# Samples' scores in halves of two units, eleven buffers of gathered latents, and rotary gathers queued behind the latents' gathers

## The chip, the core and the metric

The kernel runs on one core of a Trainium2 chip: TensorE (PE in the profile, its weight loads PEld), VectorE (DVE), ScalarE (ACT), GpSimd (POOL), SyncE (SP) and sixteen DMA engines. The metric is device time in microseconds; less is better. The kernel before took 1371.54 us (median of three runs, 1371.13 to 1372.58).

## The reference

One inference step of a two-layer decoder for a prompt of 1024 tokens (and 16 meta tokens) and for eight requests of four new tokens each ("samples"). The samples attend to a paged cache of 2048 past positions each. For a request, with its pages gathered by the page table:

```python
q_lat = einsum('blhd,chd->blhc', q_nope, w_uk)          # 16 heads x 4 tokens = 64 rows, 256 latent columns
keys  = concat([past_c, past_kr])                       # 256 latent + 32 rotary columns, 2048 positions
s     = (q_lat . latents + q_rope . rotary keys) * SCALE
p     = softmax(s)
o_lat = p @ latents                                     # 64 x 256
o     = einsum('blhc,chv->blhv', o_lat, w_uv)
y     = x + rmsnorm((o * silu(z)) @ w_out_mla)
```

The prompt goes through the same layer with ordinary keys and values, and both streams share the output weights. Everything is float32; the kernel splits each operand into a rounded high part and the rest, and multiplies high x high, high x low and low x high.

## The kernel before

The program is traced in Python and then put in order by a scheduler, which runs a simulation of the engines and, on each engine, takes the instruction that is ready, earliest in program order first. A tile can be allocated only when a buffer of its tag is free. Pools stand one behind the other in each partition of the on-chip memory; a pool opened after another was closed takes the same bytes, and its instructions wait for the last use of what lay there.

The prompt's attention ends near 1105 us. Its pool `wq` (L669) holds per partition: `raw` 2 x 6144 bytes, `ph` (tag wh) 4 x 2048, and `pl` (tag wl) 4 x 2048. `ph` and `pl` are the high and low part of the probabilities (`parts`, L1195), made for each unit of each head and read by `values` (L1213) three units later, to the last unit of the last head.

The samples' stage begins at L1306. Pool `sc` (7424 bytes) takes the bytes from where `wq` began; then stand, in this order, `sw`, `sg`, `sk`, `sch`, `scn0`, `sn` and `scn1`:

- `sw` (22592 bytes): `ot` 1024, the scores `st` 2 x 8192, `m` 2 x 32, `pt` 2 x 2560.
- `sg` (768 bytes): the page table (L1318), `crow`, `ktab`, `krow`, `krun`: the rows to gather. The page table is one load (L1319), `ktab` eight (L1328); VectorE makes `krow` (L1330) and `crow` (L1333) of them.
- `sk`: `kn`, `kx`, `kh`, `kl` (one buffer each) and `kp` (five): gathered rotary keys, transposed, split, and moved to the layout of a matmul.
- `scn0` and `scn1`: `cn`, the gathered latents, 3 and 6 buffers of 4096 bytes.

The work is 32 units: request b, quarter g of its positions (512 of them). The loop (L1545) goes in steps; at step s it calls

- `gather` (L1393) of unit s+5: an indirect DMA issued by GpSimd, 512 KB into `cn`;
- `rotary` (L1374) of the request whose first unit is s+4: an indirect DMA into `kn`, and SyncE's twelve DMAs to `kp`;
- `take` (L1399) of unit s+1: eight transposes on TensorE, split by ScalarE (`ch`) and VectorE (`cl`);
- `scores` (L1414) of unit s: five matmuls, the one with `kp` among them, and VectorE's sum into `st`; after the fourth unit of a request `softmax` (L1426);
- `turn` and `halve` (L1438, L1457) of unit s-5, `weigh` (L1467) of unit s-6: the probabilities transposed (`pt`), the latents split (`nh`, `nl`, after which `cn` is free), eight matmuls; `close` (L1482) ends a request;
- and, from step 5 on, a share of `left` (L1522): the prompt's rows times the first half of the output weights, with its `gh` queued on ScalarE behind the latest `ch`. `columns` (L1502) loads and splits those weights through two `raw` buffers; `left` copies its product to `ma` and stores it.

The gathers and the rotary gathers go through `spread` (L1367), which puts each behind a later mask instruction of the last two heads on GpSimd. After the loop `uv` is loaded into a buffer of `st`, and the second half of the output weights follows (L1589).

## Time and profile before

| | |
|---|---|
| median of the runs | 1371.54 us |
| profiled execution | 1369.06 us, of which its span is 1367.3 |
| TensorE busy | 94% of the span (weight loads 85%) |
| VectorE, ScalarE, GpSimd busy | 63%, 49%, 45% |
| mean granted clock of TensorE | 0.975 of 2.4 GHz |

A row of a timeline gives the start and the length in us, the engine, the line, the operation, what it writes and reads, the count of merged instructions, and in brackets how long the engine was idle before it and what ended that. A row of busy time by stretch gives, for each engine, busy us and instructions. All times count from the start of the span.

### The profile page before, as it was taken

The page shows a single profiled execution, that of the slowest core. Times are in us where ns is not written, and L with a number is a line of the kernel's source. Part 1 is how long each engine was busy: PE and PEld are TensorE (multiplying, and loading weights), DVE is VectorE, ACT ScalarE, POOL GpSimd, SP SyncE. Part 2 cuts the span into 40 slices and gives each one's busy share as a digit, 9 for nine tenths or more (in the row PEclk, how much of TensorE's full clock was granted, in tenths as well). Part 3 has the DMA queues.
Part 4 walks back from the last instruction along what each step waited for, and adds up shares of the span by engine and source line. Part 5 has one row for each costly group of instructions (what it writes and reads, how often), then busy time and mean ns, then how long its engine had stood idle before and what let it go on. Part 6 is the DMA issues. An engine that isn't in the chain of part 4 may idle for free.

```text
span 1367.3 us, 22924 instructions
## 1 busy us (share of the span) xinstructions
PE 1291.8 (94%) x8142; PEld 1163.4 (85%) x8142; DVE 854.9 (63%) x1749; ACT 673.8 (49%) x1394; POOL 609.3 (45%) x828
## 2 busy tenths in 40 slices
PE   7799999999989999999999989999999879899988
PEld 6699999999968899999999878878888757677776
DVE  5776555666464445167523667777778669567875
ACT  5433333333243334222321566666767668678842
POOL 5456555555311133463410654655546634445421
PEclk8999999999999999999999999999999979999999
DMA  6122122122362232345610121121211276444354
GB/s 194 46 64 72 48 70 79 49 78 63 100 214 93 91 109 69 99 150 197 214 41 1 40 63 36 36 63 28 61 35 38 73 213 182 114 146 134 105 183 168
DMA packets 107149, 131.86 MB, mean 96 GB/s; under 512 B 21135, under 2 KB 80187, under 8 KB 107035
## 3 DMA queue, kind: packets, MB, share of 16 engines
q1 hardware_dynamic: 101787, 111.51, 27.6%
q0 software_dynamic: 5248, 18.88, 4.5%
q8 instruction: 65, 1.06, 0.3%
q14 instruction: 49, 0.40, 0.1%
HBM read 93.95 MB, written 28.78 MB: 90 GB/s over the span
## 4 chain that ended last, share of the span: by engine, by line
PE 74%; DMA 10%; DVE 6%; ACT 3%; issue 3%; POOL 2%; SPq 1%; DVEq 0%; POOLq 0%; ACTq 0%
PE b L69 11%; PE pa L69 10%; PE po L69 8%; PE ps L69 8%; PE c L69 7%; PE a L69 6%; PE pm L69 6%; PE pz L69 6%; DMA qh<-qd32h 3%; PE pf L69 3%; PE pr L69 3%; PE pc L1406 2%; DMA cn<-in_cache_ckv_dram,crow 1%; PE pk L69 1%; PE pt L69 1%
## 5 line engine op out<-in xcount | busy, mean ns | idle before, releaser
L79 DVE TENSOR_TENSOR wl<-raw,wh 128x512 fp32r<-128x512 f32 x86 | 70.6, 823 | 85.4 <-ACT wh L74 82.2
L74 ACT ACTIVATE wh<-raw 128x512 fp32r<-128x512 f32 x88 | 55.2, 630 | 127.7 <-PE pa L69 48.9
L1187 ACT ACTIVATE p<-ps 128x512 f32<-128x512 f32 (+1 forms) x192 | 93.4, 492 | 37.5 <-PE ps L69 33.7
L74 ACT ACTIVATE ph<-p 128x512 fp32r<-128x512 f32 (+1 forms) x192 | 97.5, 527 | 22.0 <-POOL p L1192 20.6
L69 PE MATMUL pz<-ph,v 128*128 128x512 f32 (+3 forms) x384 | 104.4, 358 | 0.4 <-ACT ph L74 0.2
L79 POOL TENSOR_TENSOR nl<-cn,nh 128x256 fp32r<-128x256 f32 x64 | 60.3, 959 | 87.3 <-ACT nh L74 63.2
L79 POOL TENSOR_TENSOR pl<-p,ph 128x512 fp32r<-128x512 f32 (+2 forms) x75 | 81.8, 1099 | 31.5 <-ACT ph L74 23.5
L79 DVE TENSOR_TENSOR pl<-p,ph 128x512 fp32r<-128x512 f32 (+3 forms) x117 | 79.1, 681 | 26.5 <-ACT ph L74 24.7
L1043 DVE TENSOR_REDUCE mx<-pm 128x1 f32<-128x16 f32 (+6 forms) x210 | 83.5, 424 | 18.9 <-PE pm L69 18.5
L1192 POOL TENSOR_SCALAR_AFFINE_SELECT p<-p 128x127 f32<-128x127 f32 (+1 forms) x128 | 48.3, 381 | 82.7 <-ACT p L1187 65.1
L69 PEld LDWEIGHTS pz<-ph,v 128*128 128x128 f32 x384 | 65.8, 192 | 7.2 <-ACT ph L74 1.2
L69 PE MATMUL pm<-kh,qh 128*128 128x144 f32 (+6 forms) x210 | 61.3, 342 | 11.0 <-DMA qh<-qd32h 10.8
L69 PE MATMUL ps<-qh,kh 97*128 97x512 f32 (+3 forms) x192 | 68.8, 358 | 2.5 <-ACT p L1187 1.3
L69 PE MATMUL pz<-pl,v 128*128 128x512 f32 (+1 forms) x192 | 68.0, 355 | 2.3 <-DVE pl L79 2.1
L69 PE MATMUL ps<-qh,kl 97*128 97x512 f32 (+3 forms) x192 | 67.5, 351 | 0.0
L69 PE MATMUL ps<-ql,kh 97*128 97x512 f32 (+3 forms) x192 | 67.3, 351 | 0.0
L69 PE MATMUL pa<-x1h,wh 128*128 128x352 f32 x288 | 64.5, 331 | 0.0
L69 PE MATMUL pa<-x1h,wl 128*128 128x352 f32 x288 | 63.9, 328 | 0.0
L69 PE MATMUL pa<-x1l,wh 128*128 128x352 f32 x288 | 62.9, 327 | 0.0
L74 ACT ACTIVATE wh<-s 128x512 fp32r<-128x512 f32 x48 | 30.0, 630 | 66.5 <-POOL s L173 25.9
L108 POOL TENSOR_SCALAR ta<-ss 128x1 f32<-128x1 f32 (+2 forms) x36 | 9.3, 257 | 118.8 <-ACT xa L623 51.7
L79 DVE TENSOR_TENSOR wl<-s,wh 128x512 fp32r<-128x512 f32 x45 | 44.4, 989 | 20.5 <-ACT wh L74 18.8
(483 smaller groups left out, 4418.7 us busy)
## 6 DMA issues: line engine op xcount, KB each, us to landing
raw<-in_w_in_conv_dram SPq DMA_DIRECT2D x32, 512.0 KB
raw<-in_w_in_mla_dram SPq DMA_DIRECT2D x12, 512.0 KB
raw<-in_w_out_conv_dram SPq DMA_DIRECT2D x8, 512.0 KB
x1d<-xa SPq DMA_DIRECT2D x8, 512.0 KB
qd64h<-qxh SPq DMA_DIRECT2D x8, 512.0 KB
qd64l<-qxl SPq DMA_DIRECT2D x8, 512.0 KB
qh<-qd64h SPq DMA_DIRECT2D x16, 256.0 KB
ql<-qd64l SPq DMA_DIRECT2D x16, 256.0 KB
```

Source lines behind the costliest of these rows:

```text
L69: return pe.matmul(out, a, b, start=start, stop=stop, **kw)
L74: return act.activation(out, src, AF.Copy, scale=scale)
L79: (eng or dve).tensor_tensor(out, src, f(hi), ALU.subtract)
L108: pool.tensor_scalar(t[:r], ss[:r], 1.0 / n, EPS, ALU.mult, ALU.add)
L1043: dve.tensor_reduce(mx[:, b, c:c + 1], pm[:, :off], AX.X, ALU.max)
L1187: act.activation(pt[:r, :n], ps[:r, :n], AF.Exp, scale=SCALE)
L1192: marks[h] = marks.get(h, []) + [pool.affine_select(pt[:r, :dn], pt[:r, :dn], [[1, dn]], ALU.is_ge, 0.0, base=META + c0 - t * P, channel_m ...
L1406: state["turned"] = pe.transpose(pc[:, r], cn[:, r, c * P:(c + 1) * P], ident)
```

## The change

The scores of a request are kept in two tiles of two units, from three buffers of half the size, in place of one tile of four units from two buffers; `softmax` and `turn` index them so, and `uv` is loaded in two halves into two of them. The latents' buffers are 3 and 8 in place of 3 and 6. From request 2 on, the rotary gather is queued on GpSimd behind the latents' gather that was traced last. The tile `ma` of `left` shares the tag, and so the two buffers, of the weights' `raw`.

```diff
--- before.py
+++ after.py
@@ -1311,9 +1311,10 @@
         sg = l9.enter_context(sbuf("sg"))
         sk = l9.enter_context(sbuf("sk"))
         sch = l9.enter_context(sbuf("sch"))
-        scn = [l9.enter_context(sbuf("scn0", bufs=CNB[0]))]
+        cnb = 3, 8
+        scn = [l9.enter_context(sbuf("scn0", bufs=cnb[0]))]
         sn = l9.enter_context(sbuf("sn"))
-        scn.append(l9.enter_context(sbuf("scn1", bufs=CNB[1])))
+        scn.append(l9.enter_context(sbuf("scn1", bufs=cnb[1])))
 
         table = sg.tile([P, NB, PAGES // 4, 4], I32, name="table")
         sp.dma_start(table.rearrange("p b g n -> p (b g n)"), i["page_table"].rearrange("b p -> (b p)").rearrange("(a n) -> a n", a=1).to_broadcast((P, NB * PAGES)))
@@ -1335,7 +1336,7 @@
         kruns = i["cache_krope"].rearrange("n (k r) d -> (n k) (r d)", r=16)
 
         def fetch(dst, src, row):
-            pool.indirect_dma_start(dst, None, src, bass.IndirectOffsetOnAxis(ap=row, axis=0))
+            return pool.indirect_dma_start(dst, None, src, bass.IndirectOffsetOnAxis(ap=row, axis=0))
 
         rr_ = sc.tile([2 * DR + 4, SEQ], F32R, tag="olt", name="rr")[2 * DR:]
         divisors(pairs[NH // 2 - 1], new, rr_)
@@ -1369,12 +1370,15 @@
             n = len(fetched) * SPN
             fetched.append(n)
             with tc.issue_after(order[min(n, len(order) - 1)]):
-                fetch(*args)
+                return fetch(*args).ins
 
         def rotary(b):
 
             kn = sk.tile([P, 16, DR], F32, tag="kn", name="kn", bufs=1)
-            spread(kn.rearrange("p r d -> p (r d)"), kruns, krow[:, b:b + 1])
+            with ExitStack() as l:
+                if b > 1:
+                    l.enter_context(tc.issue_after(state["g"]))
+                spread(kn.rearrange("p r d -> p (r d)"), kruns, krow[:, b:b + 1])
             kx = sk.tile([P, 4, 4, 32], F32, tag="kx", name="kx", bufs=1)
             dve.transpose(kx.rearrange("p a r k -> p (a r k)"), kn.rearrange("p r d -> p (r d)"))
 
@@ -1391,9 +1395,9 @@
                 state["p", b, g] = kp
 
         def gather(b, g):
-            pl = scn[(4 * b + g) % sum(CNB) >= CNB[0]]
+            pl = scn[(4 * b + g) % sum(cnb) >= cnb[0]]
             cn = pl.tile([P, 4, KV], F32, tag="cn", name="cn")
-            spread(cn.rearrange("p r c -> p (r c)"), cruns, crow[:, b, g:g + 1])
+            state["g"] = spread(cn.rearrange("p r c -> p (r c)"), cruns, crow[:, b, g:g + 1])
             state["n", b, g] = cn
 
         def take(b, g):
@@ -1419,31 +1423,31 @@
 
             t = sch.tile([DN, 512], F32, tag="t", name="t", bufs=2)
             act.activation(t, ps[DN:], AF.Copy)
-            if g == 0:
-                state["s", b] = sw.tile([P, 4, 512], F32, tag="st", name="st")
-            dve.tensor_tensor_reduce(state["s", b][:DN, g], ps[:DN], t, 1.0, NEG, ALU.add, ALU.max, tops[:, b, g:g + 1])
+            if g % 2 == 0:
+                state["s", b, g // 2] = sw.tile([P, 2, 512], F32, tag="st", name="st", bufs=3)
+            dve.tensor_tensor_reduce(state["s", b, g // 2][:DN, g % 2], ps[:DN], t, 1.0, NEG, ALU.add, ALU.max, tops[:, b, g:g + 1])
 
         def softmax(b):
-            st = state["s", b]
             m = sw.tile([DN, 2], F32, tag="m", name="m")
             dve.tensor_reduce(m[:, 0:1], tops[:, b], AX.X, ALU.max)
             dve.tensor_scalar(m[:, 1:2], m[:, 0:1], -SCALE, None, ALU.mult)
             mine = own[:, (TS + LS) * b:(TS + LS) * b + LS]
             act.activation(mine, fresh[:, b], AF.Exp, scale=SCALE, bias=m[:, 1:2], accum_out=sums[:, b, 0:1])
             for n in range(2):
-                act.activation(st[:DN, 2 * n:2 * n + 2], st[:DN, 2 * n:2 * n + 2], AF.Exp, scale=SCALE, bias=m[:, 1:2], accum_out=sums[:, b, n + 1:n + 2])
+                st = state["s", b, n]
+                act.activation(st[:DN], st[:DN], AF.Exp, scale=SCALE, bias=m[:, 1:2], accum_out=sums[:, b, n + 1:n + 2])
             dve.tensor_reduce(sums[:, b, 3:4], sums[:, b, :3], AX.X, ALU.add)
             dve.reciprocal(sums[:, b, 3:4], sums[:, b, 3:4])
 
         def turn(b, g):
 
-            st = state["s", b]
+            st = state["s", b, g // 2]
             if b == NB - 1:
                 pp = pss.tile([P, 512], F32, tag="s", name="pp")[:, :5 * DN].rearrange("p (n c) -> p n c", c=DN)
             else:
                 pp = psp.tile([P, 5, DN], F32, tag="p", name="pp")
             for n in range(4):
-                pe.transpose(pp[:, n], st[:DN, g, n * P:(n + 1) * P], ident[:DN, :DN])
+                pe.transpose(pp[:, n], st[:DN, g % 2, n * P:(n + 1) * P], ident[:DN, :DN])
             pt = sw.tile([P, 5, P], F32R, tag="pt", name="pt", bufs=PTB)
             if g == 3:
                 pe.transpose(pp[:TS, 4], own[:, TS * b:TS * b + TS], ident[:DN, :DN])
@@ -1529,7 +1533,7 @@
                     mm(po[:r], x[:, k, :r], w[k], k == 0 and n == 0, k == NK - 1 and n == 2)
                 if k % 2:
                     yield
-            a = nw.tile([P, 512], F32, tag="a", name="ma", bufs=2)
+            a = nw.tile([P, 512], F32, tag="raw", name="ma", bufs=2)
             act.activation(a[:r], po[:r], AF.Square, scale=D ** -0.5, accum_out=ss2[:r, b, 0:1])
             pool.tensor_scalar(ss2[:r, b, 2:3], ss2[:r, b, 0:1], EPS, None, ALU.add)
             act.activation(a[:r], po[:r], AF.Copy)
@@ -1567,12 +1571,13 @@
             while done < (s_ - FS) * FR:
                 next(fill, None)
                 done += 1
-        uv = sw.tile([P, 4, 512], F32, tag="st", name="uv").rearrange("p (c a) m -> p c (a m)", c=2)
-        sp.dma_start(uv, i["w_uv"].rearrange("(c p) h d -> p c (h d)", p=P))
+        uv = [sw.tile([P, 2, 512], F32, tag="st", name="uv", bufs=3).rearrange("p a m -> p (a m)") for _ in range(2)]
+        for c in range(2):
+            sp.dma_start(uv[c], i["w_uv"].rearrange("(c p) h d -> c p (h d)", p=P)[c])
         po = pss.tile([P, 8, 2 * TS], F32, tag="s", name="pu")
         for pr in range(8):
             for c in range(2):
-                mm(po[:, pr], uv[:, c, pr * P:(pr + 1) * P], olt[:, c, 2 * pr:2 * pr + 2].rearrange("p h t -> p (h t)"), c == 0, c == 1)
+                mm(po[:, pr], uv[c][:, pr * P:(pr + 1) * P], olt[:, c, 2 * pr:2 * pr + 2].rearrange("p h t -> p (h t)"), c == 0, c == 1)
         for e in range(2):
             rr = slice(e * DV, (e + 1) * DV)
             dve.scalar_tensor_tensor(zt[rr, :, SEQ:], po[rr, :, e * TS:(e + 1) * TS], 0.5, zt[rr, :, SEQ:], ALU.mult, ALU.mult)
```

## Rows read from the trace of the kernel before

**Rows 1.** Busy us by stretch: PE, PEld, DVE, ACT, POOL (instructions), clock, DMA share, GB/s

```profile
1088.00:1105.50 17.50, 15.61 (x84) 13.59 (x83) 12.39 (x22) 14.48 (x30) 9.41 (x15) 0.90 0.39 120
1105.50:1126.10 20.60, 13.21 (x59) 8.74 (x58) 14.47 (x32) 11.19 (x22) 8.07 (x9) 0.73 0.95 292
1126.10:1200.00 73.90, 66.62 (x357) 51.76 (x358) 54.85 (x115) 58.26 (x115) 31.75 (x35) 0.91 0.52 147
1200.00:1300.00 100.00, 94.79 (x568) 71.86 (x566) 74.32 (x161) 80.20 (x167) 49.95 (x55) 1.00 0.42 131
...
1311.30:1356.00 44.70, 44.68 (x212) 35.01 (x212) 29.41 (x41) 11.83 (x24) 7.55 (x13) 1.00 0.54 188
```

**Rows 2.** TensorE's waits, 1080 to 1312: us in total, times, longest us

```profile
PE pc L1406 <- DMA cn<-in_cache_ckv_dram,crow: 12.3, 7, 4.3
```

**Rows 3.** TensorE's timeline: transposes of gathered latents that waited

```profile
1088.98 1.09 PE L1406 MATMUL pc<-ident,cn 128*128 128x128 f32 x8 [0.95 <-DMA cn<-in_cache_ckv_dram,crow]
...
1115.37 1.97 PE L1406 MATMUL pc<-ident,cn 128*128 128x128 f32 x8 [4.32 <-DMA cn<-in_cache_ckv_dram,crow]
...
1190.21 1.12 PE L1406 MATMUL pc<-ident,cn 128*128 128x128 f32 x4 [2.28 <-DMA cn<-in_cache_ckv_dram,crow]
...
1214.93 1.09 PE L1406 MATMUL pc<-ident,cn 128*128 128x128 f32 x8 [1.91 <-DMA cn<-in_cache_ckv_dram,crow]
...
1237.27 1.09 PE L1406 MATMUL pc<-ident,cn 128*128 128x128 f32 x8 [0.97 <-DMA cn<-in_cache_ckv_dram,crow]
...
1271.80 1.10 PE L1406 MATMUL pc<-ident,cn 128*128 128x128 f32 x8 [0.95 <-DMA cn<-in_cache_ckv_dram,crow]
```

**Rows 4.** GpSimd's timeline, 1083 to 1109: gathers of latents (cn) and rotary keys (kn)

```profile
1083.94 1.54 POOL L1338 DMA_INDIRECT cn<-in_cache_ckv_dram,crow  x1 [1.18 <-DVE crow L1333]
...
1093.69 1.41 POOL L1338 DMA_INDIRECT kn<-in_cache_krope_dram,krow  x1 [0.97 <-DVE krow L1330]
...
1101.53 1.21 POOL L1338 DMA_INDIRECT kn<-in_cache_krope_dram,krow  x1 [0.16 <-issue]
...
1103.21 0.95 POOL L1338 DMA_INDIRECT cn<-in_cache_ckv_dram,crow  x1 [0.17 <-issue]
1106.92 0.95 POOL L1338 DMA_INDIRECT kn<-in_cache_krope_dram,krow  x1 [2.76 <-DVE kx L1379]
...
1108.38 0.95 POOL L1338 DMA_INDIRECT cn<-in_cache_ckv_dram,crow  x1 [0.16 <-issue]
```

**Rows 5.** The chain of waits in order of time: start us, us, what

```profile
1113.78 9.67 DMA rr<-rl
...
1185.22 4.94 DMA cn<-in_cache_ckv_dram,crow
```

**Rows 6.** SyncE's timeline: the page table's load

```profile
1079.53 0.43 SPq L1319 DMA_DIRECT2D table<-in_page_table_dram  x1
```

**Rows 7.** VectorE's timeline: rows to gather; a score that waits for a buffer

```profile
1082.58 1.06 DVE L1333 TENSOR_SCALAR crow<-table,run 32x32 int32<-32x32 int32 x4 [0.92 <-DMA table<-in_page_table_dram]
...
1181.34 0.68 DVE L1424 CUSTOM_DVE_ANT_0 st<-ps,t 64x512 f32<-64x512 f32 x1 [4.82 <-PE pp L1446]
```

**Rows 8.** TensorE's timeline: scores with kp of units 0, 4, 8; a late pl matmul

```profile
1103.59 0.40 PE L69 MATMUL ps<-kp,qp__5572 96*64 96x512 f32 x1
...
1104.53 0.35 PE L69 MATMUL pz<-pl,v 128*128 128x400 f32 x1
...
1127.57 0.63 PE L69 MATMUL ps<-kp,qp__5572 96*64 96x512 f32 x1
...
1144.83 0.40 PE L69 MATMUL ps<-kp,qp__5572 96*64 96x512 f32 x1
```

**Rows 9.** Costliest groups, 1126 to 1300: weight splits on VectorE (count, busy us, mean ns)

```profile
L79 DVE TENSOR_TENSOR wml<-wor,wmh 128x512 fp32r<-128x512 f32 x13 | 9.6, 749 | 2.2 <-ACT wmh L74 2.0
```

**Rows 10.** Timelines of SyncE and ScalarE: second half's weights; the last `ma`

```profile
1283.76 8.30 SPq L1507 DMA_DIRECT2D wor<-in_w_out_mla_dram  x4
...
1289.89 0.57 ACT L1533 ACTIVATE ma<-pf 128x512 f32<-128x512 f32 x1
```

## Prediction

> **What bounds the kernel now.** The page first: TensorE is busy for nearly the whole span, so a change can win or lose only where TensorE idles or runs at the lower of its two clock levels. Then the busy time by stretch, for the stage that the diff touches [rows 1]. Busy time taken from the length gives the idle time, and one less the granted clock, times the busy time, gives roughly what the lower level costs. From 1088.0 to 1105.5 (the last attention head, with the samples' first pieces in it): 1.9 us idle and 0.10 x 15.6 = 1.6 us of clock. From 1105.5 to 1126.1: 7.4 and 0.27 x 13.2 = 3.6. From 1126.1 to 1200: 7.3 and 0.09 x 66.6 = 6.0. From 1200 to 1300: 5.2 and none. After 1311.3 TensorE is busy for 44.68 of 44.70 us, so what the samples' stage loses moves the end one for one. In the stretches from 1126.1 to 1300 18.5 us stand to be won, and no more.
>
> Then the list of waits, for TensorE alone: the largest is the transposes of `take` waiting for gathered latents, 12.3 us in seven waits [rows 2]. In order of time [rows 3] they are 0.95 us before 1089.0 (a second like it follows), 4.32 before 1115.4, 2.28 before 1190.2, 1.91 before 1214.9, 0.97 before 1237.3 and 0.95 before 1271.8. The one before 1115.4 has a plain cause in GpSimd's timeline [rows 4]: kn of request 1 at 1101.5, then a gather at 1103.2 that is already the tenth unit's (it goes into the buffer of unit 0, which is free), then kn of request 2, which sat 2.76 us until VectorE had transposed the kn before it out of the single buffer, and only at 1108.4 the gather of unit 3, which TensorE needs next. The later ones come from the nine buffers: `gather` of unit v needs the buffer of unit v-9, which `halve` frees a step after the gather's place in the loop. In the chain of waits such a gather lands 4.9 us after its issue [rows 5].
>
> **The change part by part.** *Eleven buffers.* `gather(v)` now needs unit v-11, freed a step before its place, some two steps (of 4.3 us or more, below) sooner, which is more than the 4.9 us of a landing. So the four waits after 1126 go: 2.28 + 1.91 + 0.97 + 0.95 = 6.1 us, and some clock: behind the 2.28 four transposes took 1.12 us, as long as eight behind the 1.91 [rows 3], so 0.55 for each four, and with their other half and the matmuls after them I put 1.6 us on it: **-7.7 us**. What is late next in that stretch is the work of VectorE and ScalarE (54.9 and 58.3 of 73.9 us, then 74.3 and 80.2 of 100, [rows 1]).
>
> *Rotary gathers behind the latents'.* This takes the 2.76 us and two issues of kn out from ahead of units 3 to 8, and by itself would end the 4.32 us wait. A later kn costs nothing by itself: behind the gather of unit 4b+1 it is still issued some four steps before the scores of unit 4b. But the gain only counts if the opening stays as it is, and that is the next part.
>
> *What the smaller score buffers move.* This is the term that decides. The pools stand one behind the other. `wq` of the attention and `sc` of the samples begin at the same byte. In `wq`, 12288 bytes of raw and 8192 of ph come first, then four slots of pl, bytes 20480 to 28672. Behind `sc` (7424 bytes) stands `sw` with 22592 (1024 + 2 x 8192 + 64 + 2 x 2560), so `sg`, the pool of the page table and of all rows to gather, begins at 30016, clear of pl by 1344 bytes. With three halves of 4096 in place of two wholes `sw` has 18496, and `sg` begins at 25920: inside the third pl slot, with krow, krun and the first kn reaching into the fourth. All four pl slots rotate until the last four units of the last head. Now the page table is loaded at 1079.5 [rows 6], while attention runs, and units 0 to 2 are gathered from 1083.9 and transposed from 1089.0 [rows 3, 4]. After the change that load can't go before a pl slot has been read for the last time; the last but one such read is at 1104.5 [rows 8].
>
> What is serial behind that load: page table 1079.53, rows at 1082.58 [rows 7], first gather 1083.94, first transpose 1088.98; beside it the eight ktab loads and krow, kn at 1093.69, its transpose, its halves and their way to kp, and the first score with kp at 1103.59 [rows 3, 4, 6 to 8]. That is 24.1 us from the load to the first score, and today attention hides it. From below: about 3 of the 24 are SyncE and VectorE being busy with attention, which leaves 21. From above: up to eleven gathers now run at once where three did, and at a DMA share of 0.95 [rows 1] one small load took 9.67 us [rows 5], against 3.05 us for the page table (1079.53 to 1082.58); one such delay makes it 30. I take 24, since the two effects work against each other. Attention ends sooner without the samples' pieces in it: 24 transposes, 3.3 us at 1.09 for eight, two gather waits of 0.95 [rows 3], and some clock, so the slot is free near 1099 instead of 1104.5, and the first score comes near 1123 instead of 1103.6. TensorE has only the transposes of three units in that hole; `left` can't fill it, because its gh is queued on ScalarE behind the latents of a later unit.
>
> Not all of the 20 us is lost, because the kernel before then loses time itself: its unit 4 is scored with kp only at 1127.57 [rows 8]. After the change units 0 to 3 have their latents at hand, and go at 3.5 to 4.3 us each (4.3 is the mean from unit 4 at 1127.57 to unit 8 at 1144.83, [rows 8]), so unit 4 comes between 1137 and 1140: **+11 us** (from +7 with a hole of 21 to +17 with one of 30). Some of the eight weight splits that `columns` puts on VectorE (0.75 us each, [rows 9]) move into the hole: **-1**.
>
> At this point a rule can be weighed. The rows show a small load that takes three times as long at a full DMA share. The Trainium skill, "DMA: Bandwidth & Descriptors", section "SWDGE vs HWDGE vs iDMA", says that each DMA engine goes round-robin between the queues that the hardware and the software path feed. By that the small loads of SyncE would not stand behind a burst of gathers, the hole would be 21 us and the term +7; the 9.67 us speaks against it, though it doesn't settle which queue was ahead.
>
> *Scores by two units.* The first score of a request had to wait for the turn of the unit five before it, and in the worst case VectorE stood 4.82 us for it [rows 7]. Now that holds for every second unit, with the same five units of lag, but each half is free sooner. From below -2 (part of that stall goes), from above +6 (six more such waits at 1 us, each of which holds the cl behind it on VectorE): I take **+1.5**, because TensorE has other work queued while VectorE stands.
>
> *`ma` shares the two raw buffers.* Nothing collides until the second half of the output weights is loaded from 1283.8, while the last `ma` is written at 1289.9 [rows 10]. It holds one of two buffers for some 4 us, its store included, and the remaining weights are then loaded one at a time. Below 0 (VectorE sets the pace of the splits), above +4; I take **+1**, since TensorE already has other blocks' work. The two smaller loads in place of one for `uv` are hidden: it is used only behind the last `close`.
>
> Sum: -7.7 + 11 - 1 + 1.5 + 1 = **+4.8 us**. The profiled execution took 1369.06 us, its span 1367.3 and 1.8 around it; the sum makes 1373.9 of it. The median of the runs is 2.5 above the profiled one, so the forecast is 1371.5 + 4.8, rounded to **1376.5 us**.
>
> **Rivals.** *The buffers win (faster).* The gather waits are only the visible end of one loop, halve, gather, take, and a broken loop gives more than its waits: the other 5 us of idle and the lower clock between 1126.1 and 1200 go as well. Of 18.5 us 14 are won, and with a hole at its short end (+8) the time is about 1366. It decides if the first score comes before about 1120. For it: the clock is down behind the 2.28 us [rows 3]. Against it: from 1200 on only 5.2 us are idle at all. The Trainium skill, "Trainium Kernel Development and Optimization", section "Best Practices", says that consistent bubbles can mean that SBUF ran out; by that rule this rival is the right reading.
>
> *The hole is longer.* The ktab loads, kn and kp each land behind the burst of eleven gathers, the first score comes near 1130, and the halves of the scores add waits: +18 - 7.7 + 2.5 = +13, about 1384.5. For it: the DMA share of 0.95. Against it: each gather takes GpSimd about 1 us to issue [rows 4], so the burst builds up slowly.
>
> *The change does not delay the page table.* If the load still goes out while attention runs, no hole opens, and only gains are left: 7.7, the 4.3 before 1115.4, and some clock: about 1359. The byte offsets speak against it.
>
> **How the numbers follow.** Forecast 0.50 (1370 to 1383), buffers win 0.25, longer hole 0.17, no delay 0.08. The range leaves out the last and the upper half of the longer hole: 1361 to 1387. A measurement of this kernel can tell about 0.2%, 2.7 us, from no change. Faster: 0.03 of the forecast, 0.20 of the first rival, 0.08 of the last, 0.31. Same: 0.13 + 0.05 = 0.18. Slower: 0.34 + 0.17 = 0.51.
>
> **What would show it.** Right: the page table's load in SyncE's timeline behind the last pl matmul, near 1099; the first `take` near 1108, the first kp score near 1123; TensorE mostly idle between; no gather wait of TensorE after that; all gathers of units 3 to 10 ahead of kn of request 2 on GpSimd. Wrong: a page table loaded near 1079, a kp score before 1115, or TensorE's idle time between 1140 and 1300 unchanged or larger, which would make the score halves the new wait.

## The result

The changed kernel takes 1416.5 us (median of five runs, 1412.3 to 1419.5) against 1371.54: a ratio of 1.0327, 95% interval 1.0303 to 1.035, so 45 us slower. The forecast was 1376.5 with a range of 1361 to 1387: the sign was right, the size was not. The profiled execution took 1413.45 us, its span 1411.7; before it was 1369.06 and 1367.3 [rows 1 to 10 are from that one].

To see where 44 us of span went, I cut both spans at three starts and the end: VectorE's last fold of the row maxima in attention (`mr`, called the mark; TensorE has run 6759 matmuls up to it before and after), the kp matmul of unit 4, and that of unit 31. All numbers of this kind below are differences of such starts.

| us | to the mark | opening: mark to unit 4 | stage: unit 4 to unit 31 | tail: unit 31 to the end |
|---|---|---|---|---|
| before | 1078.5 | 49.1 | 152.9 | 86.8 |
| after | 1079.2 | 66.7 | 170.9 | 94.8 |
| difference | +0.7 | +17.6 | +18.0 | +8.0 |

So three stages lost time, where the forecast had one. First the opening. The timelines of SyncE, GpSimd, VectorE and TensorE of the changed kernel (start us, length, instruction, idle time before it and what ended that):

```profile
1096.54 0.36 SPq L1320 DMA_DIRECT2D table<-in_page_table_dram  x1
...
1101.02 1.25 POOL L1339 DMA_INDIRECT cn<-in_cache_ckv_dram,crow  x1 [3.33 <-DVE rc L1084]
...
1113.76 0.94 POOL L1339 DMA_INDIRECT cn<-in_cache_ckv_dram,crow  x1 [0.30 <-issue]
...
1116.96 0.97 POOL L1339 DMA_INDIRECT kn<-in_cache_krope_dram,krow  x1 [0.16 <-issue]
...
1125.61 0.71 DVE L1383 STREAM_TRANSPOSE kx<-kn 128x512 f32<-128x512 f32 x1 [2.56 <-DMA kn<-in_cache_krope_dram,krow]
...
1132.61 0.66 PE L69 MATMUL ps<-kp,qp__5572 96*64 96x512 f32 x1 [9.91 <-DMA kp<-kl]
```

The page table is loaded 17 us later than in [rows 6], behind attention, as forecast. But the eleven latent gathers (the first and the last stand here, one every 1.25 us) all go out ahead of the first rotary gather, which had only three ahead of it in [rows 4]. It is issued 20.4 us behind the page table (14.2 before) and is used 8.65 us after its issue (1097.39 less 1093.69, 3.70, before), so the chain from table to first kp score is 36.1 us where [rows 6] and [rows 8] give 24.1. Of the 12.0 us more, 6.3 lie before the issue (1.9 of them before VectorE has its rows, `krow`, ready) and about 5 between issue and use. The use in the kernel before:

```profile
1097.39 0.71 DVE L1379 STREAM_TRANSPOSE kx<-kn 128x512 f32<-128x512 f32 x1 [1.01 <-DMA kn<-in_cache_krope_dram,krow]
```

The busy time of the same stretches (length, then PE, PEld, DVE, ACT, POOL with their instructions, granted clock, DMA share, GB/s), after:

```profile
1096.50:1132.60 36.10, 10.78 (x42) 7.52 (x42) 13.16 (x27) 9.14 (x16) 17.29 (x23) 0.59 0.66 228
1132.60:1146.00 13.40, 9.01 (x38) 6.17 (x39) 7.87 (x15) 8.28 (x14) 0.07 (x1) 0.72 0.44 119
...
1146.00:1316.90 170.90, 153.55 (x830) 116.27 (x831) 115.07 (x248) 122.61 (x247) 69.45 (x79) 0.90 0.40 116
```

and before:

```profile
1103.60:1127.60 24.00, 16.59 (x71) 10.87 (x70) 15.82 (x36) 13.86 (x28) 8.63 (x10) 0.74 0.90 278
...
1127.60:1280.50 152.90, 141.31 (x815) 108.92 (x814) 112.98 (x241) 122.00 (x245) 72.55 (x81) 0.96 0.47 138
```

Read by the prediction's own rule (idle, and clock as one less the granted clock times busy), the stage had 11.6 us idle and 5.7 of clock, and has 17.4 and 15.4: about 6 us of idle and 10 of clock, 16 of the 18; the stage also holds 830 matmuls for 815. VectorE's and TensorE's waits of the changed kernel, 1080 to 1360 (us in total, times, longest):

```profile
DVE st L1428 <- PE pp L1450: 23.0, 12, 4.2
...
PE pc L1410 <- DMA cn<-in_cache_ckv_dram,crow: 10.8, 3, 7.4
PE ps L69 <- DMA kp<-kl: 10.6, 2, 9.9
```

The seven gather waits of [rows 2] have become three: 7.4 us in the opening, and 3.3 us behind it instead of 6.1. So the eleven buffers did halve the wait that they were counted for, and the stage still became longer: TensorE idles more for other reasons, and its clock is lower. Four slices of the stage after (the same columns as above):

```profile
1246.00:1250.00 4.00, 4.00 (x25) 3.08 (x24) 2.70 (x9) 3.41 (x9) 1.67 (x3) 1.00 0.65 210
1250.00:1254.00 4.00, 2.35 (x13) 1.72 (x13) 1.53 (x4) 3.96 (x10) 1.30 (x2) 0.86 0.51 185
1254.00:1258.00 4.00, 4.00 (x20) 3.35 (x19) 2.90 (x6) 2.58 (x6) 2.87 (x4) 0.50 0.01 2
1258.00:1262.00 4.00, 4.00 (x24) 2.97 (x22) 2.59 (x8) 2.18 (x6) 1.95 (x2) 0.79 0.63 197
```

and two slices of before around its longest gap between 1195.8 and 1269.4, the 1.91 us ahead of 1214.93 in [rows 3]:

```profile
1210.50:1214.20 3.70, 2.52 (x16) 1.50 (x14) 3.70 (x8) 2.70 (x6) 3.28 (x4) 1.00 0.67 195
1214.20:1217.90 3.70, 2.97 (x23) 2.63 (x23) 2.24 (x7) 2.48 (x4) 0.19 (x1) 1.00 0.50 155
```

After, TensorE stands for 1.65 us in one piece, and the granted clock is at the lower level (0.50, 1.2 GHz) in the whole next slice. Near 1231 and 1281 it falls again (0.72 and 0.65 in slices of 3.9 us), about once per request of four units. But a gap alone does not bring the lower level. Before stands longer, 1.91 us, and its clock is 1.00 in every slice from 1195.8 to 1269.4; its 2.28 us ahead of 1190.21 were followed by slow transposes [rows 3]. What decides between the two is not shown here. That the change costs clock is sure all the same: the mean granted clock of a whole execution was 0.957 to 0.959 in the five of the changed kernel, and 0.967 to 0.986 in those of the kernel before.

What stands around the gap of 1.65 us, in the timelines of VectorE, ScalarE and TensorE after:

```profile
1246.09 0.68 DVE L1428 CUSTOM_DVE_ANT_0 st<-ps,t 64x512 f32<-64x512 f32 x1 [1.81 <-PE pp L1450]
...
1246.70 0.68 DVE L1428 CUSTOM_DVE_ANT_0 st<-ps,t 64x512 f32<-64x512 f32 x1
...
1247.82 0.15 DVE L1433 TENSOR_SCALAR m<-m 64x1 f32<-64x1 f32 x1
...
1249.36 1.14 ACT L1438 ACTIVATE st<-st,m 64x1024 f32<-64x1024 f32 x1
...
1250.49 1.14 ACT L1438 ACTIVATE st<-st,m 64x1024 f32<-64x1024 f32 x1
...
1251.62 0.58 ACT L74 ACTIVATE ch<-pc 128x512 fp32r<-128x512 f32 x1
...
1252.98 0.69 PE L69 MATMUL ps<-cl,qs 128*64 128x512 f32 x1 [1.66 <-DVE cl L79]
```

Two units' scores wait for one turn and are then taken together. The request's last scores come late by that, the maximum and both exponentials follow at once, and ScalarE's `ch` for the next latents, which TensorE needs, stands behind the exponentials. This is one gap in one profile.

The tail, in SyncE's timeline after, against [rows 10], where the second half of the output weights goes out from 1283.76:

```profile
1305.98 0.34 SPq L1511 DMA_DIRECT2D wor<-in_w_out_mla_dram  x1
1326.72 0.33 SPq L1576 DMA_DIRECT2D uv<-in_w_uv_dram  x1
1330.29 0.33 SPq L1540 DMA_DIRECT2D md<-ma  x1
1331.23 1.43 SPq L1511 DMA_DIRECT2D wor<-in_w_out_mla_dram  x2
```

One weight load goes early, and the second only when the last `ma` has left the shared buffer, 25 us later. The load of `uv`, which waits for a score half, stands in between.

### The profile page after: what moved, and what is told of

It reads as the page before. It is cut to its first block, busy times and chain, and to the rows that moved or that the text cites. A ratio compares the mean times of both kernels' runs of the same rounds, so it can differ in the third digit from the quotient of the medians.

```text
span 1411.7 us, 22955 instructions
## 1 busy us (share of the span) xinstructions
PE 1309.3 (93%) x8142; PEld 1174.0 (83%) x8142; DVE 856.9 (61%) x1749; ACT 672.9 (48%) x1394; POOL 604.6 (43%) x828
## 3 DMA queue, kind: packets, MB, share of 16 engines
q0 software_dynamic: 5248, 18.88, 4.2%
## 5 line engine op out<-in xcount | busy, mean ns | idle before, releaser
L79 POOL TENSOR_TENSOR pl<-p,ph 128x512 fp32r<-128x512 f32 (+2 forms) x75 | 81.7, 1097 | 31.4 <-ACT ph L74 24.1
L108 POOL TENSOR_SCALAR ta<-ss 128x1 f32<-128x1 f32 (+2 forms) x36 | 8.3, 231 | 123.8 <-ACT xa L623 51.5
L1410 PE MATMUL pc<-ident,cn 128*128 128x128 f32 x256 | 44.5, 314 | 15.9 <-DMA cn<-in_cache_ckv_dram,crow 10.8
```

The lines of the kernel that those rows point to most:

```text
L79: (eng or dve).tensor_tensor(out, src, f(hi), ALU.subtract)
L108: pool.tensor_scalar(t[:r], ss[:r], 1.0 / n, EPS, ALU.mult, ALU.add)
L1410: state["turned"] = pe.transpose(pc[:, r], cn[:, r, c * P:(c + 1) * P], ident)
```

## Experiments

Every kernel below ran beside the kernel before on the same chip. Two limits to reading them. One profile gives a section only so well: the same program, profiled twice (*e_rotary* and *e_rotary_again*), had stages of 149.5 and 155.1 us and openings of 49.3 and 47.0. The clock makes the difference of the stages: they were granted 0.99 and 0.94, which is 1.4 and 8.7 us by the rule above, and had 10.8 and 9.7 us idle. And the time up to the mark, in which nothing differs, went from 1071.1 to 1082.2. So verdicts go by the ratios, and sections only tell where.

| kernel | parts | ratio to before (95%) | opening | stage | tail |
|---|---|---|---|---|---|
| before | | 1 | 49.1 | 152.9 | 86.8 |
| e_rotary | rotary order | 0.9963 (0.9938 to 0.9988) | 49.3 | 149.5 | 88.9 |
| e_rotary_again | the same | 0.9979 (0.996 to 0.9997) | 47.0 | 155.1 | 89.4 |
| e_rotary_own | rotary order, tied to the own request | 0.9956 (0.9933 to 0.9978) | 50.2 | 148.0 | 89.6 |
| e_halves | three halves | 1.0052 (1.0032 to 1.0072) | 51.7 | 152.7 | 90.0 |
| e_four_halves | four halves | 1.0015 (0.9995 to 1.0034) | 51.5 | 151.6 | 88.9 |
| e_four_rot | four halves, rotary order | 0.9994 (0.9977 to 1.0011) | 49.3 | 157.2 | 88.8 |
| e_shared | shared raw buffers | 1.0026 (1.0005 to 1.0047) | 51.3 | 151.4 | 92.4 |
| e_hole | low page table | 1.0213 (1.0177 to 1.0248) | 60.1 | 153.6 | 104.9 |
| e_hole2 | low page table, other place for `pt` | 1.0153 (1.0116 to 1.0191) | 60.3 | 155.6 | 95.6 |
| e_ten_plain | ten buffers, shared raw | 1.0145 (1.0118 to 1.0172) | 50.8 | 160.8 | 97.0 |
| e_four_ten | ten buffers, shared raw, four halves | 1.0098 (1.0068 to 1.0129) | 53.2 | 152.8 | 96.3 |
| e_ten | ten buffers, shared raw, rotary order | 1.0182 (1.0133 to 1.023) | 52.1 | 167.1 | 96.4 |
| e_no_share | ten buffers, three halves, rotary order | 1.0146 (1.0108 to 1.0183) | 53.9 | 169.0 | 92.9 |
| e_nine | three halves, shared raw, rotary order | 1.0029 (1.0011 to 1.0047) | 48.0 | 153.1 | 95.2 |
| e_relaid | after, page table at its old byte | 1.0176 (1.0138 to 1.0214) | 54.3 | 164.7 | 96.0 |
| e_no_rotary | e_relaid without the rotary order | 1.0159 (1.0117 to 1.02) | 53.1 | 170.3 | 95.4 |
| e_after_nine | after with nine buffers | 1.0228 (1.0199 to 1.0256) | 61.5 | 160.8 | 96.4 |
| e_kn_first | after, first rotary gather early | 1.0292 (1.0267 to 1.0317) | 62.3 | 171.7 | 95.9 |
| after | all | 1.0327 (1.0303 to 1.035) | 66.7 | 170.9 | 94.8 |

### The low page table

*e_hole*: the kernel before, with page table, row numbers and rotary buffers at the changed kernel's bytes.

```
         sw = l9.enter_context(sbuf("sw", bufs=2))
+        gap = l9.enter_context(sbuf("gap")).tile([P, 272], F32, name="gap")
         sg = l9.enter_context(sbuf("sg"))
         sk = l9.enter_context(sbuf("sk"))
+        sw2 = l9.enter_context(sbuf("sw2", bufs=2))
         sch = l9.enter_context(sbuf("sch"))
...
-            m = sw.tile([DN, 2], F32, tag="m", name="m")
+            m = sw2.tile([DN, 2], F32, tag="m", name="m")
...
-            pt = sw.tile([P, 5, P], F32R, tag="pt", name="pt", bufs=PTB)
+            pt = sw2.tile([P, 5, P], F32R, tag="pt", name="pt", bufs=PTB)
```

> The kernel before, with nothing changed but where tiles lie: a gap and the probability buffers change places with the page table and the rotary buffers, so that these start at the byte they have in the changed kernel, under the last low halves of phase one's weights. Scores, gathers' buffers and the order of the code stay. Theory A (three separate costs: opening, score halves, tail): the first rotary score comes 20 to 29 us later than before's 1103.6, unit 4 at 1141 to 1147, and from unit 4 on everything takes what it took before (152.9 us to unit 31, 86.8 us from there to the end): 1385 to 1391 us. Theory B (the opening is all of it, the rest of the 45 us follows from starting late and cold): 1410 to 1418 us, with the later stages longer as in the changed kernel. Theory C (the prediction's chain of 24 us holds where only nine gathers stand ahead of the rotary one, and eleven are what made it 36): first rotary score near 1123, 1378 to 1383 us.

Measured: +29 us (2.13% of 1371.5). The opening is 11.0 us longer, the prediction's +11, though by other steps: the first score comes 49.1 us behind the mark, where the forecast's 1123 is 44.5, and unit 4 11.1 us behind it, where it had 14 to 17; the two misses cancel. The stage is as before. The tail is 18 us longer, and none of the theories had that; *e_hole*'s edit had put `pt`, which is read until the end, under the second half's weights. So it was made once more with `pt` behind the gather buffers (`sw2` placed after `scn1`, the rest as above).

> As the run that put the page table and rotary buffers at the changed kernel's bytes in the kernel before, but with the probability buffers behind the gather buffers, so that they do not lie where the second half of the output weights goes. If that place made the tail of 104.9 us: opening 60 us, stage 153 us, tail 87 to 90 us, ratio 1.008 to 1.011. If the late opening itself makes the tail (weight loads behind other loads in the queue): tail 95 us and more, ratio 1.014 and more.

Measured: +21 us, opening +11.2 again, tail 95.6: still 8.8 longer than before's. SyncE's timeline of *e_hole2* at its end:

```profile
1298.99 0.38 SPq L1573 DMA_DIRECT2D uv<-in_w_uv_dram  x1
1308.23 4.32 SPq L1509 DMA_DIRECT2D wor<-in_w_out_mla_dram  x3
```

Unit 31 is scored at 1286.9 there, so these loads go 21 us behind it, and behind `uv`; in [rows 10] the first four go 3 us behind unit 31, and `uv` only at 1295.3. SyncE itself waited 8.8 us before 1308.23, for VectorE's `wml`: the two raw buffers were still full. ScalarE starts to split the second half's weights, which empties them, 19.6 us behind unit 31 in *e_hole2* and 1.2 us behind it (1280.5) in the kernel before:

```profile
1306.56 1.14 ACT L74 ACTIVATE wmh<-wor 128x512 fp32r<-128x512 f32 x2
...
1281.67 1.14 ACT L74 ACTIVATE wmh<-wor 128x512 fp32r<-128x512 f32 x2
```

That late split is a second price of the low page table, which the forecast did not have. Why the planner places it so late is not shown.

*e_relaid* is the reverse: the changed kernel with one gather buffer moved between the scores' pool and the page table, which brings that back to its old byte.

```
         sw = l9.enter_context(sbuf("sw", bufs=2))
+        scl = l9.enter_context(sbuf("scl"))
         sg = l9.enter_context(sbuf("sg"))
...
-        cnb = 3, 8
+        cnb = 3, 7
...
-            pl = scn[(4 * b + g) % sum(cnb) >= cnb[0]]
+            n = (4 * b + g) % 11
+            pl = scl if n == 10 else scn[n >= cnb[0]]
```

> The changed kernel with one of its eleven gather buffers put between the scores' buffers and the page table, so that table and rotary buffers lie at before's bytes again; all else is as changed. Theory A: opening as before's (first rotary score near 1104, unit 4 at 1127 to 1130), the halves' waits and the longer tail stay: 1395 to 1401 us. Theory B (the opening is all): 1364 to 1372 us. If the late opening had hidden a part of the halves' cost (the gathers were then ahead), it gives 1402 to 1408 us.

Measured: +24 us, 21 less than the changed kernel. The opening (54.3) is 5 us longer than before's, the stage still 11.8, the tail 9.2. So the opening is not all (theory B falls), and something in the stage is left.

*e_kn_first* asks why the opening is 17.6 and not 11 longer: in the changed kernel, gathers from the fourth on are put behind the first rotary gather.

```
+        state["k0"] = state["k"]          # the instruction of rotary(0)'s gather
...
-            state["g"] = spread(cn.rearrange("p r c -> p (r c)"), cruns, crow[:, b, g:g + 1])
+            with ExitStack() as l:
+                if b or g == 3:
+                    l.enter_context(tc.issue_after(state["k0"]))
+                state["g"] = spread(cn.rearrange("p r c -> p (r c)"), cruns, crow[:, b, g:g + 1])
```

> The changed kernel with the first request's rotary gather ahead of the fourth latent gather on the gather engine; no buffer changes. Theory G: the chain from the page table's load to the first rotary score shrinks from 36 us to 26 to 30, unit 4 comes 4 to 8 us earlier, what comes behind stays as slow, ratio to before 1.027 to 1.031 (the changed kernel has 1.033). Rival (the gathers pushed back are then what is late): unit 4 no earlier, ratio 1.032 to 1.036.

Measured: ratio 1.0292, 5 us less than the changed kernel; opening 62.3. Timelines of GpSimd and VectorE of *e_kn_first*:

```profile
1110.10 0.97 POOL L1339 DMA_INDIRECT kn<-in_cache_krope_dram,krow  x1 [0.57 <-DVE krow L1331]
...
1114.16 0.71 DVE L1383 STREAM_TRANSPOSE kx<-kn 128x512 f32<-128x512 f32 x1 [1.26 <-DMA kn<-in_cache_krope_dram,krow]
```

The rotary gather goes 14.6 us behind the page table (1095.49), as before, and is used 4.06 us after its issue instead of 8.65. Table to first score is 28.6 us here, 31.9 and 32.0 with nine gathers ahead (*e_hole2*, *e_after_nine*), 36.1 with eleven. So 4.4 of the remaining 6.6 us of the opening are the rotary gather's place behind the latents' in GpSimd's queue, and behind their data.

### The number of gather buffers

*e_nine* has all of the change's other parts, with before's layout; *e_relaid* differs from it by two more buffers.

```
-            a = nw.tile([P, 512], F32, tag="a", name="ma", bufs=2)
+            a = nw.tile([P, 512], F32, tag="raw", name="ma", bufs=2)
...
+        gap = l9.enter_context(sbuf("gap")).tile([P, 1024], F32, name="gap")     # behind sw
...                                        (and the halves and the rotary order of the change)
```

> The kernel before with three halves, the shared raw buffers and the new order of the rotary gathers, but nine gather buffers, every tile of the opening at its old byte. Theory E (the buffers cost the 12 us): unit 4 to unit 31 152 to 155 us, VectorE's waits for the turns near the 11 us of the halves alone, in all 1375 to 1382 us. Theory D (the rotary order): 162 us and more, in all 1385 to 1392 us. The tail after unit 31 is 93 to 97 us if the shared raw buffers make it, 90 if the halves do.

Measured: 1.0029, stage 153.1. Three halves, shared buffers and rotary order together cost 4 us; the two more buffers of *e_relaid* cost 20. The buffers, the part from which the gain was to come, are the dearest beside the low page table. *e_no_rotary* and *e_no_share* take the rotary order and the shared buffers out of it (the latter with ten buffers, since there is no room for eleven):

```
             with ExitStack() as l:
-                if b > 1:
-                    l.enter_context(tc.issue_after(state["g"]))
                 spread(kn.rearrange("p r d -> p (r d)"), kruns, krow[:, b:b + 1])
```

> The re-laid kernel (halves in three buffers, eleven gather buffers, shared raw buffers, page table at before's bytes) without the new order of the rotary gathers. The re-laid kernel was 24.5 us over before: about 5 in the opening, 12 between unit 4 and unit 31 (164.8 us against 152.9), 9 after unit 31. Theory D (late rotary gathers make VectorE wait for them, which costs the 12): unit 4 to unit 31 takes 152 to 156 us, in all 1378 to 1383 us. Theory E (eleven buffers let takes go ahead of the turns, so that the third half is waited for): 162 to 166 us, in all 1388 to 1393 us.

> The kernel before with three halves, ten gather buffers (the tenth in the bytes that the halves give back) and the new order of the rotary gathers; the copies of the left-hand blocks keep their own buffers. Theory F (sharing the raw buffers makes the longer tail): from unit 31 to the end 89 to 91 us as with the halves alone, against 96.0 of the re-laid kernel. Theory D or E for the stage before it: unit 4 to unit 31 162 to 166 us, ten buffers being as good as eleven for going ahead. In all 1381 to 1386 us; if sharing plays no part 1388 to 1393 us.

Measured: 1.0159 and 1.0146, stages of 170.3 and 169.0: neither the rotary order nor the sharing makes the stage long. That left halves and buffers together. *e_ten* and *e_ten_plain* have whole scores, ten buffers (`cnb = 3, 7`) and the shared buffers that make room, with and without the rotary order:

> The kernel before with ten gather buffers, shared raw buffers and the new order of the rotary gathers, but whole score tiles of four units in two buffers; the opening's tiles at their old bytes. If the halves are what the buffers and the order run against (theory A in its new form: costs only together): unit 4 to unit 31 148 to 153 us, in all 1366 to 1374 us with the tail of the shared buffers in it. If buffers or rotary order cost by themselves: 160 us and more for that stage, in all 1380 to 1388 us.

> The kernel before with ten gather buffers and the shared raw buffers that make room for the tenth; whole score tiles, rotary order and layout of before. If more gather buffers cost by themselves: unit 4 to unit 31 164 us and more (before 152.9), ratio 1.013 and more. If they cost only together with the halves or with the rotary order: 150 to 155 us for that stage, 5 to 9 us in the tail for the shared buffers, ratio 1.002 to 1.006.

Measured: 1.0182 and 1.0145. So it isn't the halves either: ten buffers in the kernel before, with the shared buffers (3.6 us by themselves, *e_shared*), cost 20 us. Between the profiles of *e_shared* and *e_ten_plain* 9 us more lie in the stage and 5 in the tail. ScalarE, GpSimd and TensorE of *e_ten_plain* where its worst gap lies:

```profile
1194.55 1.14 ACT L1435 ACTIVATE st<-st,m 64x1024 f32<-64x1024 f32 x1
...
1195.68 1.14 ACT L74 ACTIVATE nh<-cn 128x512 fp32r<-128x512 f32 x2
...
1196.38 1.85 POOL L79 TENSOR_TENSOR nl<-cn,nh 128x256 fp32r<-128x256 f32 x2 [3.82 <-ACT nh L74]
1198.38 0.95 POOL L1339 DMA_INDIRECT cn<-in_cache_ckv_dram,crow  x1 [0.15 <-PE po L69]
...
1202.96 1.97 PE L1407 MATMUL pc<-ident,cn 128*128 128x128 f32 x8 [3.17 <-DMA cn<-in_cache_ckv_dram,crow]
```

With ten buffers the gather still goes out directly behind the `nl` that frees its buffer, and that `nl` waits for `nh`, which stands behind a request's exponentials on ScalarE. TensorE then waits 3.17 us for it in one piece; in this kernel's stage the gather waits are 12.6 us in eight, against before's 6.1 in four. The slices around it:

```profile
1199.00:1203.00 4.00, 0.50 (x5) 0.36 (x5) 1.38 (x4) 2.07 (x5) 3.30 (x5) 0.68 0.76 219
1203.00:1207.00 4.00, 4.00 (x19) 3.47 (x20) 2.10 (x7) 1.40 (x4) 0.00 (x0) 0.50 0.37 125
```

Here 3.5 us without work are followed by 4 us at the lower level of the clock. *e_four_ten* tests whether the scores' next tile is what the further-ahead gathers run into: four halves of 4096 bytes (`bufs=4`, before's bytes) are written again only after the turn of the unit seven earlier.

> The kernel before with four score halves, ten gather buffers and the shared raw buffers that make room for the tenth; rotary order and layout of before. If the buffers cost because the scores' next tile then waits for the turns (three halves or two whole tiles): with four halves there is no such wait, unit 4 to unit 31 148 to 153 us, ratio 1.000 to 1.005. If more buffers cost whatever the scores' tiles: 163 us and more, ratio 1.012 and more.

Measured: stage 152.8, opening 53.2, tail 96.3, ratio 1.0098, between the two expectations. In its profile the stage's loss is gone with four halves, and the run is 6 us under *e_ten_plain*, though the two intervals overlap a little: the scores' next tile is likely a part of the cause. But the interval (+9 to +18 us) leaves some 4 us and more above what shared buffers and four halves cost alone (3.6 and 2), so more buffers gain nothing with them either. *e_after_nine* does the same undoing in the changed kernel itself (`cnb = 3, 6`):

> The changed kernel with nine gather buffers in place of eleven and nothing else undone (halves, shared raw buffers, rotary order and the low page table stay). Against the same parts with the table at its old byte (1.003 of before) it differs by the opening alone. Theory G (two large costs: the buffers' number and the opening): the opening adds 11 to 14 us, the stage from unit 4 to unit 31 takes 152 to 156 us against the changed kernel's 170.8, in all 15 to 22 us over before (ratio 1.011 to 1.016). Rival (the opening also spoils the stage behind it): unit 4 to unit 31 165 us and more, ratio 1.022 and more.

Measured: 1.0228, 14 us less than the changed kernel, 5 of them in the opening, 10 in the stage. That is the rival's ratio, and not theory G's. Against *e_nine* (1.0029), the same kernel with the page table at its old byte, it is 27 us longer, the low page table's price once more (21 in *e_hole2*, 29 in *e_hole*). Its stage of 160.8 is 8 us longer than that of *e_nine* and holds 836 matmuls for 817, so a part of it is work that moved in from the opening; how much I leave open, one profile being good for 6 us or so.

One number separates the kernels better than the stage's length does, TensorE's idle time in the stage: 8.8 to 13.7 us in the twelve profiles with nine buffers, 17.4 to 23.7 in seven with ten or eleven, and 13.6 in *e_four_ten*. What the clock cost there does not separate them (0 to 10 us with nine, 6 to 17 with more).

### Halves, shared buffers, rotary order

*e_halves* is the scores' part alone, with a gap of 4096 bytes behind `sw`; *e_four_halves* the same with `bufs=4` and no gap.

```
-            if g == 0:
-                state["s", b] = sw.tile([P, 4, 512], F32, tag="st", name="st")
+            if g % 2 == 0:
+                state["s", b, g // 2] = sw.tile([P, 2, 512], F32, tag="st", name="st", bufs=3)
...                                        (readers and uv as in the change)
```

> The kernel before with only the scores in halves of two units, three buffers, and w_uv loaded in two halves; a gap of 4096 bytes keeps every other tile where it was. Theory A: the opening is before's (first rotary score 1103 to 1104, unit 4 at 1127 to 1128), but VectorE waits with every second score unit for TensorE's transposes of the unit five earlier, some 13 us per two units, and unit 31 comes 14 to 20 us later than before's 1280.5: 1386 to 1393 us. Theory B (the opening is all): within 3 us of before, 1369 to 1375 us, with the waits of VectorE short. The prediction on record had +1.5 us (-2 to +6) for this step.

> The kernel before with the scores in halves of two units and four buffers: the same bytes as before's two buffers of four units, so the same layout. A half is then written again only after the transposes of the unit seven earlier, where before's first unit of each request, and every second unit with three halves, waits for the unit five earlier. Theory A (the number of halves is what costs, not the halving): VectorE's waits for TensorE's transposes go, 1366 to 1371 us. Rival (the halving itself costs, by the split load of w_uv or another order of the work): 1378 us or more, near what three halves give.

Measured: +7 us (4.4 to 9.9) with three, +2 (-0.7 to 4.7) with four. The 14 to 20 us in the stage that I expected of three halves, from the changed kernel's 23 us of such waits, are not there (152.7). VectorE's waits for turns are 11.2 us in six in that stage against 6.9 in two before, and TensorE has other work meanwhile. A long wait of VectorE alone was no reason for the time.

*e_shared* is the one-line edit of `ma` alone.

> The kernel before with nothing changed but the copies of the left-hand blocks sharing the two buffers of the output weights. All runs that share them have a tail of 94.8 to 97.0 us from unit 31 to the end, those that do not 86.8 to 92.9. If the sharing alone makes it: opening and the stage to unit 31 as before (49 and 153 us), tail 93 to 97 us, ratio 1.004 to 1.007. If it takes more gather buffers or halves too: tail 87 to 90 us, ratio below 1.003.

Measured: 1.0026 (1.0005 to 1.0047), tail 92.4 us, between the two expectations. SyncE's timeline of *e_shared* shows what after showed: one weight load early, the next behind the last `ma`:

```profile
1267.93 0.34 SPq L1507 DMA_DIRECT2D wor<-in_w_out_mla_dram  x1
1286.77 0.32 SPq L1536 DMA_DIRECT2D md<-ma  x1
1288.39 0.81 SPq L1507 DMA_DIRECT2D wor<-in_w_out_mla_dram  x2
```

The rotary order alone, the same again, and a variant tied to the own request's first gather (`issue_after(state["g", b, 0])`), because with nine buffers the last gather written is unit 9's, which takes unit 0's buffer and goes out ahead of units 3 to 8:

> The kernel before with nothing changed but the order of the rotary gathers of the third request and later behind the latents' gathers. The prediction took the 2.8 us wait in the opening out of the way by it: unit 4 2 to 3 us earlier after the mark in phase one than before's 49.1 us, ratio 0.997 to 1.000. If late rotary gathers cost by themselves, the stage from unit 4 to unit 31 is 156 us and more and the ratio 1.002 and more; with nine buffers I expect 151 to 155 us.

> The kernel before with the rotary gathers of the third request and later tied behind the gather of their own request's first unit, not behind the last gather written. With nine buffers the last gather written (unit 9) took unit 0's buffer and went out ahead of units 3 to 8, so the rotary order alone left the third request's rotary gather ahead of them; here it stands behind unit 8. If the prediction's step holds (its 2.8 us wait goes): unit 4 2 to 3 us earlier than with the rotary order alone, ratio 0.993 to 0.997. If that wait was covered: opening 49 to 50 us as before, ratio 0.996 to 0.999.

> The kernel before with the rotary order alone, timed once more beside its variant, since it is the best of many runs: 0.996 of before if the gain is real, 0.998 to 1.001 if it was chance.

Measured: 0.9963, 0.9956 and 0.9979, all intervals below 1: 3 to 6 us faster than before. This is the one part that helps. *e_rotary_own* has the lowest ratio of the study, but its interval overlaps those of the other two. With it the opening's gather waits are 3.3 us, the longest 2.0, against 4.32 for one in [rows 3]:

```profile
PE pc L1409 <- DMA cn<-in_cache_ckv_dram,crow: 3.3, 3, 2.0
```

Yet the opening isn't shorter (50.2), and in the first variant the third request's rotary gather still waited 2.0 us ahead of the latents'. If they gain in the stage, the profiles do not show it (149.5 and 155.1 for the same program; 148.0). So the gain is shown, its place is not.

> The kernel before with four score halves and the new rotary order, nine gather buffers, old layout: the parts that cost nothing so far, put together as the best version that the runs point to. Opening 46 to 50 us, stage 151 to 153 us, tail 88 to 89 us: ratio 0.997 to 1.002. If the two disturb each other as halves and more buffers did: 1.005 and more.

Measured: 0.9994, no difference from before that can be told: with four halves the gain of the rotary order is not seen.

## Why the forecast was right in sign and wrong in size

Taken one by one, the parts cost: low page table +21 us (*e_hole2*), buffers +16 (*e_ten_plain* less *e_shared*), halves +7, shared buffers +4, rotary order -3 to -6. That adds up to +42 to +45, and 45 were measured, but the agreement is in part luck. By section the same runs add up to about +15, +8 and +25 us for opening, stage and tail, where the changed kernel has +17.6, +18.0 and +8.0. Other pairs of runs price the page table at 27 and 29 us (*e_after_nine* less *e_nine*; *e_hole*) and the buffers at 8 to 20. So the parts act on each other: that the low page table and the buffers are the two large costs is shown, their exact shares are not. The prediction's terms against that:

- *Eleven buffers*, -7.7: **the step that failed.** Measured +8 to +20 (*e_four_ten* less its other parts; *e_relaid* less *e_nine*). The argument took the waits of [rows 3] away and left all else in its order. With eleven the named waits did go down, from 6.1 to 3.3 us; with ten they grew to 12.6 (*e_ten_plain*). In both, TensorE's idle time in the whole stage grew, from 11.6 to 17.4 and 17.9 us, and in the changed kernel's profile the lower clock cost some 10 us more on top. A reason that fits is that every engine's order is made when the program is planned, so that a buffer more moves all of it; no run tests that by itself. Where the idle time comes from is seen only for the gaps above, one in each of two kernels, and the scores' next tile has a likely part in it (*e_four_ten*); as a general cause it stays open.
- *What the smaller score buffers move*, +11 and -1: the mechanism was right (table at 1096.5 for 1099, first take at 1105.6 for 1108). That its opening alone came out at the forecast's size (*e_hole* +11.0, *e_hole2* +11.2) is luck in part, since a later first score and a shorter way from there to unit 4 cancel. The -1 was not tested. Two things were left out. The chain from table to first score is 31.9 us with nine gathers ahead of the rotary one and 36.1 with the changed kernel's eleven, not 24, and outside the bounds of 21 and 30. The prediction had counted what eleven gathers do to a landing, and in its sum not who stands ahead of whom; it had the row for it, kn behind three gathers, in [rows 4]. And the second half's weights are split later: +9 in the tail of *e_hole2*.
- The rule of the Trainium skill that was weighed there, queues served in turn ("DMA: Bandwidth & Descriptors", "SWDGE vs HWDGE vs iDMA"), would have made the hole 21. Most of what the rotary gather lost, it lost behind other gathers: the profile lists one software queue, and its 18.88 MB are those of all 32 gathers of latents and all 8 rotary ones. On such a queue a rule about turns between queues says nothing.
- *Scores by two units*, +1.5 (-2 to +6): +7 (4.4 to 9.9). Mis-sized, just outside its bounds; little of it is the wait that was argued, since the stage alone did not grow.
- *`ma` shares the raw buffers*, +1 (0 to +4): +3.6 (0.7 to 6.4), by the mechanism that was named, weights loaded behind the last `ma`. Rightly bounded, too low.
- *Rotary order*, counted at nothing since the hole would swallow it: -3 to -6 by itself. In the changed kernel with the old layout, taking it out changed nothing that can be told (1.0159 against 1.0176).

Of the rivals, the longer hole came nearest: its first score "near 1130" was 1132.6, its +18 for the opening 17.6. It was priced at 1384.5 because it too took -7.7 for the buffers. The first rival, for which the Trainium skill's remark spoke that consistent bubbles can mean that SBUF ran out ("Trainium Kernel Development and Optimization", "Best Practices"), is refuted by *e_ten_plain* and *e_four_ten*: more SBUF for the buffers did not take the bubbles away. Of the marks set for a right forecast the late page table, the first take and the order of the gathers came as named; the first kp score did not, nor did the gather waits vanish (3.3 us). Of the marks for a wrong one, one was met: TensorE's idle time from 1140 to 1300 grew, from 12.5 to 14.8 us, and in the whole stage from 11.6 to 17.4. Its reading, that the score halves would be the new wait, holds for the gap shown in the changed kernel, and not by itself as the cause: the halves with nine buffers don't lengthen the stage.

## What to carry over

Where a planner deals out buffers and orders every queue, a buffer more can change much more than the one wait that it is meant to remove: try it alone before it is counted, and price it from both sides of zero. When a buffer shrinks, follow the bytes of all that lies behind it, and then the order of the queue that the delayed load feeds, to its last member. Look at the clock of the slice that follows a gap, and not only at the sum of the waits, but do not price it from one profile: two of the same program differed by 7 us there. And when single parts add up to the total, add them up by section too before you believe it.

## What was not expected of the hardware

Two gaps of TensorE, 1.65 us (changed kernel, 1250 to 1254) and 3.5 us (*e_ten_plain*, 1199 to 1203), were each followed by a 4 us slice at a granted clock of 0.50, but one of 1.91 us in the kernel before was followed by slices at 1.00. A rotary gather behind eleven gathers of latents was used 8.65 us after its issue, and one behind three of them after 3.70 us in the kernel before and 4.06 us in *e_kn_first*.
